# Moving layer 1's adaLN products from TensorE in the mixers to VectorE in the dense feed-forward

## The chip, the cores and the metric

The kernel runs on one core of a Trainium2 chip. The metric is the device time of one execution in microseconds (us); less is better.

## The reference

Two layers of a conditioned decoder trunk, in float32, on 256 tokens of width 1024. Each layer has a mixer (retention, an S5 state-space layer and multi-head latent attention beside each other) and a feed-forward: dense in layer 0, the top 2 of 8 routed experts in layer 1. A vector `c` of length 1024 modulates both (adaLN):

```python
cond = jax.nn.silu(c)
for layer in range(DEPTH):
    mod = (cond @ ada_w[layer] + ada_b[layer])[:, None, :]      # ada_w[layer]: 1024 x 6144
    sh_m, sc_m, gt_m, sh_f, sc_f, gt_f = jnp.split(mod, 6, axis=-1)
    h = rms_norm(x, norm_pre_mix[layer]) * (1.0 + sc_m) + sh_m
    y = hybrid_mixer(h, ...)
    x = x + gt_m * rms_norm(y, norm_post_mix[layer])
    h = rms_norm(x, norm_pre_ffn[layer]) * (1.0 + sc_f) + sh_f
    y = swiglu(h, ...) if layer % 2 == 0 else routed_ffn(h, ...)
    x = x + gt_f * rms_norm(y, norm_post_ffn[layer])
```

The change concerns `cond @ ada_w[1]`, a vector times a matrix of 24 MB.

## The kernel before

**Stages.** One program, in this order: the layer-0 mixer (to about 209 us), the dense feed-forward of layer 0 (to about 454), the layer-1 mixer with routing (to about 610), and the experts (to the end). There is no loop at run time; every instruction is written out, and each engine runs its own list in order. The lists come out of the order in which the Python code emits work.

**Loads.** All weights come as 1 MB pieces (`st`, 128x2048) into five staging buffers (`NS = 5`). A first, dry pass over the code notes the order in which pieces are asked for; `pump` then issues each load, from SP's queue, in that order, as soon as a buffer has been given back (`done`). A piece that is held long holds up all loads behind it.

**Weight splits.** A weight piece is split in halves of 128x1024 (128x896 for some of the input projection): ScalarE casts the high part (`wh`, L273), VectorE subtracts for the low part (`wl`, L274), up to five halves ahead (`NH = 5`); the second half's split gives the staging buffer back. Each product is then three matmuls: in `first` L1305 to L1307, elsewhere L733 to L735 (`mm3`).

**adaLN pieces.** `ada_steps(l, u)` gives ten steps for a third `u` of a layer's modulation: eight pieces, `total` and `fin`. The piece `k` takes 128 rows of `ada_w`; four matmuls (L474) multiply it by `c` (32 equal columns `c32`) and sum it up in a bank of PSUM. `total` adds the bias and multiplies by a gain on VectorE; `fin` turns the row into columns with four small matmuls (L490) and sends rows to all partitions. The steps stand in `self.queue`; `bg` takes the next one. The mixers call it at the letter B of their order strings `ORDER0`, `ORDER1`; at a mixer's end what is left over `keep` is run. In before, four pieces of (1,0) run at the end of the layer-0 mixer and four at the entry of the feed-forward (`self.bg(4)`), its `total` and `fin` in the first chunk; the steps of (1,1) and (1,2) run at the entry of the layer-1 mixer and inside it. The `fin` of (1,2) is followed by `fold_router` (L1380 to L1384).

**Mixer parts that are named.** `turn_x` (L681) transposes the tokens 0 to 127 (t=0) or 128 to 255 (t=1) with a diagonal `dg` (L674) that holds the norm; `hh`, `hl` are the parts of the normed input. In the attention (MLA), ScalarE copies the scores (`pe`, L1111), VectorE masks them and takes the maximum, ScalarE takes the exponential (L1118), PE transposes it (L1129), ScalarE copies that (`pT`, L1130), and PE multiplies by the values (L1136).

**Dense feed-forward.** Seven chunks `c` of 512 hidden columns. For each: `first('fg', c)`, Silu, `first('fu', c)`, the product `sg` and its parts `hTh`, `hTl`, and then `down(c - 1)`, which adds the chunk before into four banks. `down_last(6)` comes after the loop, with the post norm of the first 128 tokens. Meanwhile `adv` runs `s5_prep(1)`, in which GpSimd prepares the S5 layer of layer 1 with some small VectorE operations (`s5q`, `wp`, `s5r`, `R`).

Of the kernel before, what the change touches and what calls it, by code (L numbers as in the profile page):

```python
# [226 lines left out]
class Kernel:  # L227
# [226 lines left out]
    def ada_steps(self, l, u):  # L454
# [4 lines left out]
        def piece(k):  # L459
            def f():  # L460
                if k == 0:
                    state['p'] = self.bank("d")
                    if u == 0:
                        self.m4 = self.adp.tile([128, 512], F32, name="m4")
                        src = self.a['post_gain'][l]
                        self.nc.gpsimd.dma_start(self.m4, src[:, None, :].to_broadcast([4, 32, 512]))
                        if l == 0:
                            self.load_bias(0, 0)
                    if (l, u) != (L - 1, 2):
                        self.load_bias(*((l, u + 1) if u < 2 else (l + 1, 0)))  # L470
                key = ('ada', l, u, k)
                st, = self.stream.get(key, self.a['ada_w'][l, u, k], (1, 2048))
                for g in range(4):
                    self.T.matmul(state['p'][32 * g:32 * g + 32, :], self.c32[:, k, :],  # L474
                                  st[:, 0, g * 512:(g + 1) * 512], start=(k == 0), stop=(k == 7),
                                  skip_group_check=True)
                self.stream.done(key)
            return f

        def total():  # L480
            r = state['r'] = self.b4.pop((l, u))
            self.V.tensor_add(r, state['p'], r)
# [3 lines left out]
        def fin():  # L486
            r = state['r']
            pcs = self.bank("b")
# [787 lines left out]
    def ffn_dense(self, l, side=None):  # L1276
# [13 lines left out]
        def adv(n):  # L1290
            for _ in range(n):
                if side is not None:
                    next(side, None)

# [24 lines left out]
        def down(c):  # L1319
            for i in range(2):  # L1320
# [6 lines left out]
                self.w_done(key)  # L1327
            hT.pop(c)
# [15 lines left out]
        for c in range(NC):  # L1344
# [6 lines left out]
            adv(1)  # L1351
            pu = first('fu', c)
# [8 lines left out]
            adv(1)  # L1361
            if c == 0:
                self.bg()
            else:
# [3 lines left out]
                adv(2)  # L1368
        down_last(NC - 1)
# [514 lines left out]
    def run(self, upto=9):  # L1884
        tc = self.tc
        with ExitStack() as ctx:
# [11 lines left out]
            with ExitStack() as c5:  # L1898
# [18 lines left out]
                with ExitStack() as c1:  # L1917
                    self.pools(c1, dict(h8=2, f4=6, f2=6, f1=3))
                    self.queue += self.ada_steps(1, 2)
# [12 lines left out]
    def first_layer(self, upto):  # L1932

        with ExitStack() as c1:
            self.pools(c1, dict(h8=2, f4=6, f2=6, f1=3))
            self.setup()
            self.queue = self.ada_steps(0, 0) + self.ada_steps(0, 1) + self.ada_steps(0, 2) \
                + self.ada_steps(1, 0)
            self.keep = 6
# [7 lines left out]
        with ExitStack() as c1:  # L1947
            self.pools(c1, dict(h8=2, f4=4, f2=8, f1=1))
            self.load_layer(1, self.nc.gpsimd)
            side = self.s5_prep(1, self.G, self.G, self.G)  # L1950
            self.queue += self.ada_steps(1, 1)
            self.ffn_dense(0, side)
# [27 lines left out]
```

## Time and profile before

| | |
|---|---|
| median of 3 runs | 1485.74 us (1483.95 to 1491.18) |
| the profiled execution, its own time | 1491.5 us |
| its span, first to last instruction | 1489.7 us |
| mean granted clock of TensorE | 0.968 of full speed |

Each run is one execution. The profile is of one execution whose time is that in the second line; all rows below are from it. A mean of a whole span hides that stages have different limits, so rows are given by stretch or instruction.

### The profile page before, as it was taken

How to read it: one execution, taken by the hardware profiler on the slowest of the kernel's cores; microseconds unless marked ns; L12 is line 12 of the kernel's file. 1: busy time of each engine (PE TensorE's matmuls, PEld its weight loads, DVE VectorE, ACT ScalarE, POOL GpSimd, SP SyncE). 2: the span in 40 equal slices, each digit the busy share in tenths (PEclk: the TensorE clock that was granted, in tenths of full speed). 3: DMA queues.
4: the chain of work that ended last, by engine and by line, in shares of the span. 5: the costliest groups of instructions: out<-in, count | busy, mean ns of one | idle time of the engine just before them, and what ended most of it. 6: DMA issues, size and time to landing. Idle time of an engine off the chain costs nothing. (4 is left out here: it accounts for less than half of the span.)

```text
span 1489.7 us, 21982 instructions
## 1 busy us (share of the span) xinstructions
PE 1390.6 (93%) x8563; PEld 1042.6 (70%) x8563; DVE 848.3 (57%) x1201; ACT 675.4 (45%) x936; POOL 108.9 (7%) x108
## 2 busy tenths in 40 slices
PE   4799789999998999999999999999999998999995
PEld 1676579999997867665687887755687655687652
DVE  4763556656565546313898898522797403897302
ACT  1423444444445244113787877412676202786101
POOL 3201010515021001000000000000000000000000
PEclk9899999999999999799999999999999999999998
DMA  9667794545556484699999998999999999999995
GB/s 305 245 232 277 270 311 183 183 170 172 190 196 242 183 348 184 243 424 424 425 424 403 346 375 334 365 415 425 424 425 378 365 424 425 424 425 354 376 425 207
DMA packets 70078, 482.23 MB, mean 324 GB/s; under 512 B 9800, under 2 KB 10056, under 8 KB 13008
## 3 DMA queue, kind: packets, MB, share of 16 engines
q1 hardware_dynamic: 65952, 473.69, 80.2%
q0 software_dynamic: 3024, 4.75, 1.2%
q10 hardware_dynamic: 992, 2.33, 0.5%
q8 instruction: 69, 1.13, 0.3%
q14 instruction: 41, 0.34, 0.1%
HBM read 479.66 MB, written 1.06 MB: 323 GB/s over the span
## 5 line engine op out<-in xcount | busy, mean ns | idle before, releaser
L274 DVE TENSOR_TENSOR wl<-st,wh 128x1024 fp32r<-128x1024 f32 x464 | 569.6, 1248 | 192.9 <-ACT wh L273 170.0
L273 ACT CAST wh<-st 128x1024 fp32r<-128x1024 f32 x464 | 482.9, 1052 | 274.8 <-PE a L1306 86.4
L733 PE MATMUL a<-wh,xgh 128*128 128x512 f32 x448 | 180.5, 403 | 0.0
L734 PE MATMUL a<-wl,xgh 128*128 128x512 f32 x448 | 177.3, 396 | 2.7 <-DVE wl L274 2.7
L735 PE MATMUL a<-wh,xgl 128*128 128x512 f32 x448 | 176.7, 394 | 0.0
L1593 PE MATMUL a<-st,xs 128*64 128x256 f32 x1344 | 155.1, 381 | 0.9 <-DMA st<-in_mu 0.9
L1593 PEld LDWEIGHTS a<-st,xs 128*64 128x64 f32 x1344 | 95.4, 137 | 57.4 <-issue 12.4
L1305 PE MATMUL a<-hh,wh 128*128 128x256 f32 x448 | 128.2, 286 | 1.9 <-ACT hh L710 1.2
L1743 ACT ACTIVATE sg<-a 128x256 f32<-128x256 f32 (+1 forms) x56 | 27.3, 488 | 224.1 <-PE a L1593 224.1
L1754 DVE TENSOR_TENSOR h<-sg,a 128x256 f32<-128x256 f32 (+1 forms) x56 | 30.8, 551 | 172.1 <-PE a L1593 130.1
L1306 PE MATMUL a<-hl,wh 128*128 128x256 f32 x448 | 127.6, 285 | 0.4 <-DVE hl L711 0.4
L1307 PE MATMUL a<-hh,wl 128*128 128x256 f32 x448 | 127.4, 284 | 0.0
L1610 PE MATMUL b<-st,hts 128*64 128x512 f32 x448 | 110.7, 618 | 13.8 <-ACT hts L1602 9.9
L733 PEld LDWEIGHTS a<-wh,xgh 128*128 128x128 f32 x448 | 85.6, 191 | 22.2 <-issue 2.8
L734 PEld LDWEIGHTS a<-wl,xgh 128*128 128x128 f32 x448 | 85.7, 191 | 21.0 <-DVE wl L274 4.1
L735 PEld LDWEIGHTS a<-wh,xgl 128*128 128x128 f32 x448 | 85.6, 191 | 18.5
L1305 PEld LDWEIGHTS a<-hh,wh 128*128 128x128 f32 x448 | 86.6, 193 | 2.9 <-ACT hh L710 1.4
L1306 PEld LDWEIGHTS a<-hl,wh 128*128 128x128 f32 x448 | 86.6, 193 | 0.8 <-DVE hl L711 0.6
L1307 PEld LDWEIGHTS a<-hh,wl 128*128 128x128 f32 x448 | 86.7, 194 | 0.0
L1610 PEld LDWEIGHTS b<-st,hts 128*64 128x64 f32 x448 | 34.4, 141 | 73.2 <-issue 52.2
L474 PE MATMUL d<-st,c 128*32 128x512 f32 x384 | 53.4, 656 | 23.3 <-DMA st<-in_ada_w 12.1
L337 POOL TENSOR_TENSOR pss<-pss,mhalf 128x1 f32<-128x1 f32 x8 | 5.2, 649 | 890.1 <-DVE pss L336 890.1
(424 smaller groups left out, 1993.7 us busy)
## 6 DMA issues: line engine op xcount, KB each, us to landing
st<-in_mg SPq DMA_DIRECT2D x112, 1024.0 KB, 12.9
st<-in_mu SPq DMA_DIRECT2D x112, 1024.0 KB, 11.6
st<-in_md SPq DMA_DIRECT2D x112, 1024.0 KB, 12.7
st<-in_ada_w SPq DMA_DIRECT2D x48, 1024.0 KB, 7.8
st<-in_fg SPq DMA_DIRECT2D x14, 1024.0 KB, 4.8
st<-in_fu SPq DMA_DIRECT2D x14, 1024.0 KB, 4.8
st<-in_fd SPq DMA_DIRECT2D x14, 1024.0 KB, 4.7
st<-in_w_out SPq DMA_DIRECT2D x8, 1024.0 KB, 7.2
```

The costliest lines, as they stand in the source:

```text
L273: self.S.copy(hi, src)
L274: (E or self.V).tensor_sub(lo, src, hi.bitcast(F32))
L474: self.T.matmul(state['p'][32 * g:32 * g + 32, :], self.c32[:, k, :], st[:, 0, g * 512:(g + 1) * 512], start=(k == 0), stop=(k == 7), skip ...
L733: self.T.matmul(out, xh, wh, start=start, stop=False, skip_group_check=True)
L734: self.T.matmul(out, xh, wl, start=False, stop=False, skip_group_check=True)
L735: self.T.matmul(out, xl, wh, start=False, stop=stop, skip_group_check=True)
L1305: T.matmul(o, wh[:, k, fs], hh[:, kk], start=st, stop=False, skip_group_check=True)
L1306: T.matmul(o, wh[:, k, fs], hl[:, kk], start=False, stop=False, skip_group_check=True)
L1307: T.matmul(o, wl[:, k, fs], hh[:, kk], start=False, stop=(kk == 7), skip_group_check=True)
L1593: self.T.matmul(p[64 * t:64 * t + 64, :256], x[:, 4 * i + k], w[:, k, 256 * t:256 * t + 256], start=(i == 0 and k == 0), stop=(i == 1 and ...
L1610: self.T.matmul(y[64 * i:64 * i + 64, :], ht[:, f % 2, s], ws[i][:, f], start=(first and f == 0), stop=(last and f == 3), skip_group_check ...
L1754: V.tensor_mul(h, sg, pu[:, :w])
```

## The change

The 24 pieces of layer 1 leave the queue of the two mixers. `ada_steps` gets a second form (`vec=True`), in which a piece is one VectorE instruction on 128x2048: the first one multiplies by `c` (one number for each partition), the seven behind it multiply and add to a running tile `ada` (`SCALAR_TENSOR_TENSOR`). `total` then sums over the partitions with four matmuls 32x512 against ones. 29 steps are handed to `ffn_dense`, which takes one at each of the new `step` calls and the rest ahead of `down_last`; the `fin` of (1,2) alone goes on into the layer-1 mixer. The layer-0 mixer's queue ends with layer 0's own steps, `keep` is 0, and one pool gets a third 8 KB buffer for one of 2 KB less.

```diff
--- before.py
+++ after.py
@@ -451,7 +451,8 @@
         t = self.b4[l, u] = self.adp.tile([128, 512], F32, name="b4", bufs=2)
         self.nc.gpsimd.dma_start(t, self.a['ada_b'][l, u][:, None, :].to_broadcast([4, 32, 512]))
 
-    def ada_steps(self, l, u):
+    def ada_steps(self, l, u, vec=False):
 
         state = {}
         gs = slice(64 * (u - 1), 64 * u)
@@ -459,7 +460,7 @@
         def piece(k):
             def f():
                 if k == 0:
-                    state['p'] = self.bank("d")
+                    state['p'] = None if vec else self.bank("d")
                     if u == 0:
                         self.m4 = self.adp.tile([128, 512], F32, name="m4")
                         src = self.a['post_gain'][l]
@@ -470,6 +471,14 @@
                         self.load_bias(*((l, u + 1) if u < 2 else (l + 1, 0)))
                 key = ('ada', l, u, k)
                 st, = self.stream.get(key, self.a['ada_w'][l, u, k], (1, 2048))
+                if vec:
+                    c = self.c32[:, k, 0:1]
+                    if k == 0:
+                        state['a'] = self.wkt([128, 2048], "ada")
+                        self.V.tensor_scalar(state['a'], st[:, 0], c, None, op0=OP.mult)
+                    else:
+                        self.V.scalar_tensor_tensor(state['a'], st[:, 0], c, state['a'], op0=OP.mult, op1=OP.add)
+                    return self.stream.done(key)
                 for g in range(4):
                     self.T.matmul(state['p'][32 * g:32 * g + 32, :], self.c32[:, k, :],
                                   st[:, 0, g * 512:(g + 1) * 512], start=(k == 0), stop=(k == 7),
@@ -479,13 +488,18 @@
 
         def total():
             r = state['r'] = self.b4.pop((l, u))
+            if vec:
+                state['p'] = self.bank("a")
+                for g in range(4):
+                    self.T.matmul(state['p'][32 * g:32 * g + 32, :], self.ones[:, :32],
+                                  state['a'][:, g * 512:(g + 1) * 512], start=True, stop=True, skip_group_check=True)
             self.V.tensor_add(r, state['p'], r)
             if u:
                 self.V.tensor_mul(r[gs], r[gs], self.m4[gs])
 
         def fin():
             r = state['r']
-            pcs = self.bank("b")
+            pcs = self.bank("a" if vec and u < 2 else "b")
             for i in range(4):
                 self.T.matmul(pcs[:, 4 * i:4 * i + 4], r[:, i * 128:(i + 1) * 128], self.kc[:, C_E4:C_E4 + 4],
                               start=True, stop=True)
@@ -1273,7 +1287,7 @@
         p = self.ffn_args(name, c, i, e)
         return (p[0],) + tuple(self.w_piece(*p))
 
-    def ffn_dense(self, l, side=None):
+    def ffn_dense(self, l, side=None, steps=()):
 
         V, S, T = self.V, self.S, self.T
         hh, hl = self.parts_of_h()
@@ -1291,6 +1305,11 @@
             for _ in range(n):
                 if side is not None:
                     next(side, None)
+
+        def step(n=1):
+            for _ in range(n):
+                if steps:
+                    steps.pop(0)()
 
         def first(name, c):
             p = [self.bank("a"), self.bank("a")]
@@ -1325,6 +1344,7 @@
                     if f == 1:
                         self.w_half(key)
                 self.w_done(key)
+                step()
             hT.pop(c)
 
         def down_last(c):
@@ -1349,6 +1369,7 @@
             if c == 0:
                 self.bg()
             adv(1)
+            step()
             pu = first('fu', c)
             th = self.wkt([128, 4, 256], "hTh", F32R)
             tlo = self.wkt([128, 4, 256], "hTl", F32R)
@@ -1359,6 +1380,7 @@
                 V.tensor_sub(tlo[:, 2 * b:2 * b + 2], v, th[:, 2 * b:2 * b + 2].bitcast(F32))
             hT[c] = (th, tlo)
             adv(1)
+            step(2 if c == 0 else 1)
             if c == 0:
                 self.bg()
             else:
@@ -1366,6 +1388,7 @@
                     ys.extend([[self.bank("b"), self.bank("d")], [self.bank("b"), self.bank("b")]])
                 down(c - 1)
                 adv(2)
+        step(len(steps))
         down_last(NC - 1)
 
 
@@ -1916,7 +1939,6 @@
                 self.phase += 1
                 with ExitStack() as c1:
                     self.pools(c1, dict(h8=2, f4=6, f2=6, f1=3))
-                    self.queue += self.ada_steps(1, 2)
                     self.keep = 0
                     self.mixer(1, ORDER1, {})
                     self.end_post()
@@ -1934,9 +1956,8 @@
         with ExitStack() as c1:
             self.pools(c1, dict(h8=2, f4=6, f2=6, f1=3))
             self.setup()
-            self.queue = self.ada_steps(0, 0) + self.ada_steps(0, 1) + self.ada_steps(0, 2) \
-                + self.ada_steps(1, 0)
-            self.keep = 6
+            self.queue = self.ada_steps(0, 0) + self.ada_steps(0, 1) + self.ada_steps(0, 2)
+            self.keep = 0
             self.mixer(0, ORDER0, dict(Z=self.s5_prep(0, self.V, self.G, self.V), N=self.ch_start()))
         if upto == 1:
             return
@@ -1945,11 +1966,12 @@
             self.NC = 2
         self.phase += 1
         with ExitStack() as c1:
-            self.pools(c1, dict(h8=2, f4=4, f2=8, f1=1))
+            self.pools(c1, dict(h8=3, f4=4, f2=7, f1=1))
             self.load_layer(1, self.nc.gpsimd)
             side = self.s5_prep(1, self.G, self.G, self.G)
-            self.queue += self.ada_steps(1, 1)
-            self.ffn_dense(0, side)
+            last = self.ada_steps(1, 2, True)
+            self.ffn_dense(0, side, self.ada_steps(1, 0, True) + self.ada_steps(1, 1, True) + last[:-1])
+            self.queue += last[-1:]
             self.drain(side)
         if upto in (2, 12):
             return
```

`order` below means the list in which an engine's instructions stand; `x4` is four alike in a row.

ScalarE in the attention part of the layer-0 mixer, before: the exponentials of the first 128 tokens' scores, two casts of `w_out` (`wh`), then the copies `pe` of the next scores.

```order
L1118 ACT_TABLE_LOAD
L1118 ACTIVATE pe_1202,sm<-pe_1202,mx 128x128 x4
L273 CAST wh<-st 128x1024 x2
L1111 COPY pe_1256<-b 128x2x128 x2
L1118 ACTIVATE pe_1256,sm<-pe_1256,mx 128x256 x4
L1130 COPY pT_1286<-b 128x512
L273 CAST wh<-st 128x1024 x2
L772 ACTIVATE ch<-a,pc 128x256 x2
```

The same place after:

```order
L1132 ACT_TABLE_LOAD
L1132 ACTIVATE pe_1202,sm<-pe_1202,mx 128x128 x4
L273 CAST wh<-st 128x1024 x4
L1125 COPY pe_1266<-b 128x2x128 x2
L273 CAST wh<-st 128x1024
L1132 ACTIVATE pe_1266,sm<-pe_1266,mx 128x256 x4
L1144 COPY pT_1300<-b 128x512
L786 ACTIVATE ch<-a,pc 128x256 x2
```

Two of the casts that stood behind the copy of `pT` now stand ahead of the copies of `pe`, and a fifth ahead of the exponentials.

VectorE in the last chunk of the feed-forward and up to its post norm, before (`wl` are splits, `s5q`, `wp`, `s5r`, `R` are S5 preparation, `pyg` is the post norm):

```order
L549 TENSOR_TENSOR s5q_1985<-wp 128x16
L550 TENSOR_TENSOR s5q_1986<-wp 128x16
L551 TENSOR_TENSOR wp<-s5q_1985,s5q_1986 128x16
L552 TENSOR_SCALAR wp<-wp 128x8
L274 TENSOR_TENSOR wl<-st,wh 128x1024 x4
L549 TENSOR_TENSOR s5q_1985<-wp 128x16
L550 TENSOR_TENSOR s5q_1986<-wp 128x16
L551 TENSOR_TENSOR wp<-s5q_1985,s5q_1986 128x16
L552 TENSOR_SCALAR wp<-wp 128x8
L657 TENSOR_TENSOR s5r<-s5r 128x8
L658 TENSOR_TENSOR s5r<-s5r 128x8
L660 COPY R_4074<-s5r 128x512
```

The same place after; ahead of these rows stand, after the last `hTl` and four S5 rows, one more `SCALAR_TENSOR_TENSOR` on `ada` and two `wl`. The row behind the last one is the bias sum of `total` of (1,2):

```order
L480 SCALAR_TENSOR_TENSOR ada<-st,c_108,ada 128x2048
L274 TENSOR_TENSOR wl<-st,wh 128x1024 x2
L480 SCALAR_TENSOR_TENSOR ada<-st,c_108,ada 128x2048
L563 TENSOR_TENSOR s5q_1939<-wp 128x16
L564 TENSOR_TENSOR s5q_1940<-wp 128x16
L565 TENSOR_TENSOR wp<-s5q_1939,s5q_1940 128x16
L566 TENSOR_SCALAR wp<-wp 128x8
L671 TENSOR_TENSOR s5r<-s5r 128x8
L672 TENSOR_TENSOR s5r<-s5r 128x8
L674 COPY R_4122<-s5r 128x512
L675 MEMSET R_4122 128x8
L480 SCALAR_TENSOR_TENSOR ada<-st,c_108,ada 128x2048
```

Four of the multiply-and-add instructions now stand between the last `hTl` and the post norm, with the splits and the S5 rows among them.

PE between the last `down` of the loop and `down_last`, after (before, the same rows follow each other without the L494, at L733 to L735):

```order
L747 MATMUL b<-wh,hTh 128x512
L748 MATMUL b<-wl,hTh 128x512
L749 MATMUL b<-wh,hTl 128x512
L494 MATMUL a<-ada,kc 32x512 x4
L747 MATMUL b<-wh,hTh 128x512
L748 MATMUL b<-wl,hTh 128x512
L749 MATMUL b<-wh,hTl 128x512
L747 MATMUL b<-wh,hTh 128x512
```

The four matmuls of `total` (L494) read `ada`; the matmuls of `down_last` stand behind them.

SP's loads for the last chunk, before (`fg`, `fu`, `fd` are the gate, up and down weights, `win_*` the input projection of the next mixer):

```order
L189 DMA st<-in_fg 128x2048 x2
L189 DMA st<-in_fu 128x2048 x2
L189 DMA st<-in_fd 128x2048 x4
L189 DMA st<-in_win_u 128x2048
L189 DMA st<-in_ada_w 128x2048 x5
L189 DMA st<-in_win_m 128x1792 x2
L189 DMA st<-in_win_q 128x2048 x2
```

The same place after:

```order
L189 DMA st<-in_fg 128x2048 x2
L189 DMA st<-in_ada_w 128x2048
L189 DMA st<-in_fu 128x2048 x2
L189 DMA st<-in_ada_w 128x2048
L189 DMA st<-in_fd 128x2048
L189 DMA st<-in_ada_w 128x2048
L189 DMA st<-in_fd 128x2048
L189 DMA st<-in_ada_w 128x2048 x2
L189 DMA st<-in_fd 128x2048 x2
L189 DMA st<-in_win_u 128x2048
L189 DMA st<-in_win_m 128x1792 x2
```

The pieces `ada_w` stand between the weights' loads, two of them ahead of the last two `fd`, and no longer between the loads of the input projection.

## Rows read from the trace of the kernel before

**Rows 1.** The page's busy times: us (share of the span) xinstructions.

```profile
PE 1390.6 (93%) x8563; PEld 1042.6 (70%) x8563; DVE 848.3 (57%) x1201; ACT 675.4 (45%) x936; POOL 108.9 (7%) x108
```

**Rows 2.** Busy time by stretch: PE, PEld, DVE, ACT, POOL, then PEclk, DMA share, GB/s.

```profile
209.00:443.00 234.00, 232.82 (x1688) 220.46 (x1689) 139.66 (x180) 105.81 (x122) 53.65 (x40) 0.99 0.52 186
460.00:500.00 40.00, 36.20 (x247) 31.82 (x248) 19.00 (x36) 17.19 (x32) 1.30 (x2) 0.91 0.64 227
610.00:1470.00 860.00, 831.14 (x4616) 585.58 (x4616) 496.62 (x541) 420.01 (x496) 0.70 (x1) 0.98 0.97 397
```

**Rows 3.** Costliest groups: the adaLN pieces; busy, mean ns, idle before.

```profile
L474 PE MATMUL d<-st,c 128*32 128x512 f32 x384 | 53.4, 656 | 23.3 <-DMA st<-in_ada_w 12.1
```

**Rows 4.** Timeline, end of layer-0 mixer, PE and DVE: start, us, engine, line.

```profile
203.13 1.63 PE L474 MATMUL d<-st,c 128*32 128x512 f32 x8 [2.30 <-DMA st<-in_ada_w]
204.68 3.10 PE L681 MATMUL a<-dg,x 128*128 128x128 f32 x16
...
200.92 0.29 DVE L674 TENSOR_SCALAR dg<-kc,rs 128x128 f32<-128x128 f32 x1 [0.66 <-POOL rs L337]
```

**Rows 5.** Timeline, MLA part of the layer-0 mixer, ACT and PE.

```profile
149.63 1.99 ACT L273 CAST wh<-st 128x1024 fp32r<-128x1024 f32 x2 [2.06 <-DMA st<-in_w_out]
151.53 0.64 ACT L1111 COPY pe<-b 128x256 f32<-128x256 f32 x2
...
157.88 2.08 PE L1136 MATMUL b<-vv,pT 128*128 128x128 f32 x8 [6.19 <-ACT pT L1130]
```

**Rows 6.** Timeline, DVE and POOL: sizes of operations, and one beside GpSimd.

```profile
450.37 1.41 DVE L764 SCALAR_TENSOR_TENSOR x<-pyg,pss,x 128x512 f32<-128x512 f32 x2
...
594.46 1.28 DVE L1422 SCALAR_TENSOR_TENSOR xnl<-x,rs,xnh 128x1024 fp32r<-128x1024 f32 x1
...
281.83 2.29 DVE L274 TENSOR_TENSOR wl<-st,wh 128x1024 fp32r<-128x1024 f32 x1 [1.06 <-ACT wh L273]
...
281.76 1.28 POOL L597 TENSOR_TENSOR pre<-q,q 128x512 f32<-128x512 f32 x1
```

**Rows 7.** Timeline, feed-forward, end of the fourth `down`, DVE and PE.

```profile
368.68 0.69 DVE L1359 TENSOR_TENSOR hTl<-sg,hTh 128x512 fp32r<-128x512 f32 x1 [0.69 <-ACT hTh L1358]
...
373.95 0.28 PE L1305 MATMUL a<-hh,wh 128*128 128x256 f32 x1
```

**Rows 8.** Timeline, last feed-forward chunk, DVE and PE; issue to landing of loads.

```profile
430.43 1.23 DVE L274 TENSOR_TENSOR wl<-st,wh 128x1024 fp32r<-128x1024 f32 x1 [1.65 <-ACT wh L273]
...
434.45 0.68 DVE L1356 TENSOR_TENSOR sg<-sg,a 128x512 f32<-128x512 f32 x1
...
437.79 0.69 DVE L1359 TENSOR_TENSOR hTl<-sg,hTh 128x512 fp32r<-128x512 f32 x1 [0.69 <-ACT hTh L1358]
...
445.53 0.17 DVE L549 TENSOR_TENSOR s5q<-wp 128x16 f32<-128x16 f32 x1
...
448.55 0.07 DVE L661 MEMSET R<- 128x8 f32 x1
...
443.05 0.39 PE L733 MATMUL b<-wh,hTh 128*128 128x512 f32 x1
...
st<-in_fd SPq DMA_DIRECT2D x14, 1024.0 KB, 4.7
```

**Rows 9.** Timeline, layer-1 mixer, PE.

```profile
460.03 2.02 PE L681 MATMUL a<-dg,x 128*128 128x128 f32 x16 [0.57 <-DVE dg L674]
...
466.24 0.54 PE L835 MATMUL a<-hh,wh 128*128 128x256 f32 x1 [3.20 <-ACT hh L710]
...
508.44 2.78 PE L474 MATMUL d<-st,c 128*32 128x512 f32 x24
...
558.68 1.16 PE L1136 MATMUL b<-vv,pT 128*128 128x128 f32 x8 [0.16 <-ACT pT L1130]
...
567.45 1.05 PE L490 MATMUL b<-kc,b 128*128 128x4 f32 x8 [0.83 <-ACT pT L1130]
...
569.90 3.76 PE L1136 MATMUL b<-vv,pT 128*128 128x128 f32 x16
```

## The prediction

> **What bounds the kernel now.** I read the page's busy times first: TensorE (PE) is busy 93% of the span, VectorE (DVE) 57% [rows 1]. That is a mean over stages, so I read next the busy times by stretch. In the dense feed-forward (209 to 443 us) PE is busy 232.82 of 234 us while DVE is busy 139.66, ScalarE about half and the DMA engines 0.52 of the time. In the expert stage (610 to 1470 us) PE is busy 831 of 860 us and the DMA share is 0.97 [rows 2]. The expert stage isn't touched by the change; whatever moves ahead of it moves its start and so the end. What the change can win or lose lies in the first 610 us, in two parts whose limits differ: in the feed-forward each microsecond put on PE is paid, and DVE has about 94 us to spare; in the two mixers PE has holes, in which a piece costs nothing.
>
> The third view is the costliest groups: the 48 adaLN pieces (8 matmuls in the profile each, for 4 in the code) take 53.4 us of PE, with 23.3 us of idle time before them, about half of it waits for their own load [rows 3]. A piece alone is about 1.07 us. So 24 pieces are some 26 us of PE time at most, and the timeline must say which of them PE waits for.
>
> **Part 1, the end of the layer-0 mixer (about -2).** Removed: eight pieces. Three stand in line in the output product and cost about 1.0 each; a fourth lies in a wait for DVE. The last four stand between the two transposes `turn_x`. The diagonal `dg` for the second is ready at 200.92 + 0.29 = 201.2, but the transpose starts at 204.68, because a piece ahead of it waited 2.30 us for its load [rows 4]. That is 3.5 us won; with the three, 6.5.
>
> Given back: ScalarE's order changes (the first two fences of the section on the change). With the pieces gone from the load queue the `w_out` loads come earlier in the order, so four casts `wh`, not two, stand ahead of the copy `pe` that feeds the softmax. Before, that copy came 1.9 us after the first of the casts, at 151.53; the chain behind it (scale, maximum, exponential, transpose) ended with PE waiting 6.19 us for `pT` at 157.88 [rows 5]. So this chain is the path here. The two extra casts belong to the second `w_out` load, which takes an earlier slot of SP's queue than now; from the slots I estimate its landing at 153.3 (before, a piece's load sat there), so `pe` comes near 155.4, 3.9 late, and with one `wl` more on DVE before the maximum (1.23) I subtract 4.7 altogether. Net -1.8; the bounds are -6.5 (load early, casts hidden) and 0.
>
> **Part 2, the feed-forward (about +32).** Added on DVE: 24 products of 128x2048. The trace has no such row. Nearest: the same operation at 128x512 takes 1.41 us for two, at 128x1024 it takes 1.28 [rows 6]. The slope is 0.575 per 512 columns, which gives 2.43; twice the wider row is 2.56, four slopes without any fixed part 2.3. I take 2.4. For 24 that is 57 us, inside DVE's 94 us of room, so over six chunks it is hidden: the stage's 84 half-pieces of weights (seven chunks of 12) last PE 2.9 us each, and splits (`wh`, `wl`) stand up to five halves ahead. The price if that cover goes is rival 1. Their loads, 24 MB on SP's queue, add less than half to what the DMA engines move there at 0.52. The pieces' bias rows and the finishes' rows go by POOL's queue, behind its S5 work, but are read eight steps later or in the next stage: nothing.
>
> Added on PE: three sums `total` at about 1.05 each (four matmuls 32x512, like a piece) = 3.2, and the finish of (1,1), four transposed columns of each row, about 1.0. They are in line in a stretch where PE is never idle, so both are paid.
>
> New waits of PE on DVE. `total(1,1)` stands at the end of `down(3)`, which PE ended at 373.95 in the trace. DVE ends its hT chain there at 368.68 + 0.69 = 369.4 [rows 7]; behind it stand a product (2.4), two `wl` (2.4) and the last product (2.4), so 376.5: PE waits 2.5.
>
> `total(1,2)` is the large one: `step(len(steps))` puts it on PE right before `down_last`, and PE takes its matmuls in order. On DVE it stands behind everything in the fence on VectorE: four products, the remaining `wl` and the S5 operations. Queued behind the waiting matmuls on PE are the 48 of `down_last`, whose weights are split by then, and all that follows it. I follow DVE's queue with the trace's durations. The last chunk's loads: five staging buffers, four of them held by `ada` pieces and `fd51`, so the load of `fd60` is issued only when the split at 430.43 ends (431.7), and lands after 4.7 (the median landing of such loads) at 436.4 [rows 8]. Cast 1.05 and `wl` 1.23: 438.7. The hT chain takes 4.0 us (434.45 to 438.48 in the trace) [rows 8]: 442.7. Four S5 operations, 0.6: 443.3. First product: 445.7; it frees the buffer for `fd61`, which lands at 450.4. `wl`: 446.9. Cast and `wl` of `fd61`: 452.7. Second product 455.1; two `wl` 457.5; third product 459.9; the remaining S5 operations 3.1 (445.53 to 448.62 in the trace) 463.0; fourth product 465.4. PE ended `down(5)` at 443.05 [rows 8]. So PE stands still for some 22 us. If the loads did not hold anything, the same queue without the gap for `fd61` and with `fd60` at its old time ends at about 456: a stall of 13, the lower bound of this term; the upper is 27, with the products stretched by GpSimd (below).
>
> After such a stop PE comes back at the lower of its two clock levels: after the idle time at the entry of layer 1 the stretch 460 to 500 ran at a granted clock of 0.91 [rows 2], which is 18% of 40 us at half speed, a loss of 3.6 us; here I take 3. Sum of part 2: 3.2 + 1.0 + 2.5 + 22 + 3 = +31.7.
>
> **Part 3, the layer-1 mixer (about -4.6).** Five pieces at its entry are hidden now: PE waits after them for `dg` (0.57) and for `hh` (3.20) [rows 9], so that removing them brings nothing. But the order changes: the loads no longer wait behind pieces, so three casts and three `wl` of 128x896 (about 1.1 each by the 128x1024 row) stand ahead of the second half's chain, and the finish of (1,2) with the fold of the router goes in before the second `turn_x` (about 2). I take +4.7.
>
> Inside, eight pieces stand where PE is never idle (0.93 each by the row of three: 2.78), with one `L490` of about 1: 8.4; against that I set 1.5, an estimate for three more `wl` that come ahead of the S5 scan on DVE: -6.9. Three more pieces are hidden in the softmax chain (PE waits for `pT` behind them, 0.16). At the end the finish and the router's fold move PE's L1136 from 567.45 to 569.90 [rows 9]: -2.4. Together 4.7 - 6.9 - 2.4 = -4.6; bounds -9.3 (entry hidden) and +1 (interior gains eaten by the new order of `wl`).
>
> **The sum.** -1.8 + 31.7 - 4.6 = +25.3 us. The profiled execution took 1491.5, 5.8 above the median 1485.74 of the runs (inside what they vary, 1483.95 to 1491.18); the difference is laid on the median: 1511.0.
>
> **A rule of the skill that speaks against the change.** The row: a `wl` of 128x1024 took 2.29 us while GpSimd ran a tensor operation of 1.28 us that had begun 0.07 us earlier [rows 6]; undisturbed it takes 1.23 [rows 8]. That is 1.06 lost, not a share but nearly the whole of GpSimd's instruction. The Trainium skill, "SBUF — State Buffer", section "Who interferes with whom", says that a VectorE instruction with two SBUF inputs and a GpSimd instruction that reads SBUF exclude each other for a whole instruction. By this rule, which the trace agrees with (1.28 + 1.23 - 0.07 = 2.44 against 2.29), every added product, which reads a staged piece and its running sum, pays for each GpSimd operation it meets. What that would make of the sum is the first rival, which is worked out from rows alone.
>
> **Rivals.**
> 1. *VectorE becomes the bound of the feed-forward.* GpSimd is busy 53.65 us in 209 to 443 [rows 2]. With 57 us of products DVE is at 197 of 234. Busy more than four fifths of the time, it would meet up to 45 of GpSimd's 54 us: 242, more than there is, though a part of that is in the 139.66 already. Then `wl` comes late for PE at some chunks as well. It decides when one chunk of 34 us has more than about 34 us of DVE work; the price is 5 to 15 more: 1516 to 1526. Against: five halves of splits ahead, about 11 us of slack.
> 2. *The tail stall is small and gains and losses cancel.* The change would do on balance nothing if the last products finished about when `down(5)` does. Sum without the 22 and the 3: +0.3, 1486; with the lower stall 13: 1502. For it: over 209 to 443 DVE has room. Against: the queue above is counted row by row, and four products alone are 9.6 us behind a chain ending at 442.7.
> 3. *Faster.* The stall is hidden as in 2, and the mixers give their upper bounds: -6.5 at the end of layer 0 (no late `pe`), -9.3 in layer 1, +6.7 of sums, finish and wait in the feed-forward: -9.1, 1477. It decides if the last two steps find their data ready. For it: PE is the busiest engine and 24 pieces leave it. Against: in the mixers it waited beside most of them.
>
> **How the numbers follow.** The forecast (stall 13 to 27, 1500 to 1520) gets 0.60, rival 1 0.12, rival 2 0.15, rival 3 0.13. About 0.5%, 7.4 us, is what a measurement of this kernel can tell from no change: faster (under 1478.3) 0.13, same 0.15, slower (over 1493.2) 0.72. The range 1486 to 1526 reaches down to rival 2's own time and up over rival 1; it leaves out rival 3 and the edges of 1 and 2. The forecast's own range is 1500 to 1520.
>
> **What would show it.** In the changed kernel's timeline, PE's four matmuls of `total(1,2)` wait about 22 us for `ada` from DVE, with DVE's four products spread between 443 and 465 and a wait for the cast of `fd61` in the midst; the products take 2.4 us, up to 3.6 beside GpSimd. `total(1,1)` waits 2.5 us, `total(1,0)` hardly. The second `turn_x` of layer 0 starts right after `dg`, and PE's wait for `pT` before the first L1136 grows by some 4 to 5. The expert stage keeps its length. It is wrong if the wait before `down_last` is under 10 us, or if chunks 1 to 5 of the feed-forward get longer than their sums explain.

## The result and the profile after

| | before | after |
|---|---|---|
| median | 1486.2 us (1483.95 to 1491.18, 4 runs) | 1559.97 us (1555.85 to 1562.78, 4 runs) |
| ratio | 1 | 1.048, 95% interval 1.045 to 1.051 |
| span of the profiled execution | 1489.7 us | 1558.6 us |

The change costs 74 us, about three times what was forecast (25); the range that was given ended at 1526. The page of the changed kernel has TensorE (PE) doing a little less work than before and idle for more of the span; compare [rows 1].

```profile
span 1558.6 us, 21695 instructions
PE 1387.2 (89%) x8395; PEld 1050.4 (67%) x8395; DVE 909.9 (58%) x1225; ACT 674.5 (43%) x936; POOL 123.9 (8%) x108
```

Where the 69 us of span went is read by stage. A stage is bounded by PE's first matmul of `first` and by its `turn_x` transposes in the timeline. The feed-forward is cut once more, at the end of the last `first`: ahead of it are the seven chunks, behind it the tail (`down(5)`, the last sum, `down_last`).

| stretch | before | after | difference | forecast |
|---|---|---|---|---|
| to the first matmul of the feed-forward | 209.0 | 211.8 | +2.8 | -1.8 |
| chunks 0 to 6 | 223.1 | 262.3 | +39.2 | +5.6 |
| tail | 21.8 | 52.3 | +30.5 | +26.1 |
| layer-1 mixer | 137.4 | 134.4 | -3.0 | -4.6 |
| routing, experts, end | 898.4 | 897.8 | -0.6 | 0 |

(Of the forecast's 31.7 for the feed-forward two sums, 2.1, the finish, 1.0, and a wait, 2.5, lie in the chunks, the rest in the tail.) The mixers and the tail are within 5 us of the forecast. The chunks are not: they hold 34 of the 44 us that were missed.

The busy times by stretch of the kernel after, from the layer-0 mixer's end on, one row for each stage of the table (columns as in [rows 2]):

```profile
157.00:211.80 54.80, 37.77 (x185) 30.58 (x185) 27.10 (x54) 25.49 (x61) 6.66 (x10) 0.82 0.38 144
211.80:474.10 262.30, 236.09 (x1664) 221.21 (x1665) 183.09 (x192) 99.35 (x116) 68.15 (x42) 0.93 0.65 235
474.10:526.40 52.30, 24.61 (x107) 18.67 (x107) 28.77 (x37) 10.57 (x17) 9.33 (x8) 0.74 0.48 169
526.40:660.80 134.40, 118.51 (x813) 97.19 (x812) 73.15 (x140) 57.69 (x124) 7.83 (x11) 0.91 0.37 134
660.80:1558.60 897.80, 847.60 (x4718) 600.19 (x4716) 514.13 (x583) 432.38 (x523) 3.66 (x5) 0.97 0.94 384
```

In the chunks VectorE (DVE) is busy 183 of 262 us. By that share it still has room, as before; yet PE has 26 us of holes there, where it had 1 before:

```profile
209.00:432.10 223.10, 221.92 (x1640) 211.41 (x1641) 131.42 (x168) 100.56 (x116) 49.74 (x37) 0.99 0.52 188
```

So the share doesn't tell; the waits do. The holes make 25 of the chunks' 39.2 us. The other 14.2 are PE's own busy time (236.1 against 221.9): about 3 were forecast for the sums and the finish, and the rest goes with the granted clock, 0.93 in place of 0.99. Behind a wait of 5.4 us, which is shown below, PE ran at its lower clock level; the window of the kernel after:

```profile
258.00:266.00 8.00, 4.51 (x21) 4.51 (x22) 5.70 (x4) 0.66 (x1) 0.00 (x0) 0.50 0.87 340
```

PE's waits over the span of the kernel after (what it waited for, us in total, times, longest):

```profile
PE a L494 <- DVE ada L480: 35.6, 2, 27.7
PE b L1150 <- ACT pT L1144: 14.9, 4, 12.2
PE a L1326 <- DVE wl L274: 11.3, 2, 5.9
PE d L1406 <- DVE rbs L1404: 8.2, 1, 8.2
PE a L1324 <- ACT sg L1368: 4.0, 2, 3.6
```

The first row is the two sums that were forecast to wait: 27.7 ahead of `down_last` (forecast 22, upper bound 27) and 7.9 for `total(1,1)` (forecast 2.5). The third is the one that the prediction held to be covered: weight splits that come late to PE. The fifth has the same root: the Silu (`sg`) that PE waits 3.6 us for stands on ScalarE behind a cast that waited for its load.

How they come late is seen where chunk 0 goes over into chunk 1. The timeline of the kernel after, SP, then ACT, DVE and PE:

```profile
234.50 4.15 SPq L189 DMA_DIRECT2D st<-in_fu  x2
257.94 0.33 SPq L189 DMA_DIRECT2D st<-in_ada_w  x1
...
246.19 1.05 ACT L273 CAST wh<-st 128x1024 fp32r<-128x1024 f32 x1 [9.16 <-DMA st<-in_fu]
...
247.28 1.23 DVE L274 TENSOR_TENSOR wl<-st,wh 128x1024 fp32r<-128x1024 f32 x1 [8.98 <-ACT wh L273]
248.42 0.68 DVE L1377 TENSOR_TENSOR sg<-sg,a 128x512 f32<-128x512 f32 x1
...
255.57 4.73 DVE L480 SCALAR_TENSOR_TENSOR ada<-st,c,ada 128x2048 f32<-128x2048 f32 x2
260.22 3.49 DVE L274 TENSOR_TENSOR wl<-st,wh 128x1024 fp32r<-128x1024 f32 x3
...
261.49 0.58 PE L1326 MATMUL a<-hh,wl 128*128 128x256 f32 x1 [5.41 <-DVE wl L274]
```

A `fu` load issued at 234.5 lands only at 246 (11.2 us is the median of the two `fu` loads here, 6.3 of all in this feed-forward); ScalarE's cast and VectorE's `wl` wait 9 us for it, and behind them in VectorE's order wait the chunk's product `sg`, its parts and then the two `ada` products, which start at 255.57. The pieces of these two, and a third that was issued at 233.37, hold three of the five staging buffers until then, so SP issues no load from 238.7 to 257.9. The next splits stand behind the products, and PE waits 5.4 us for `wl`. It is a ring: a held buffer makes a load late, the late load blocks VectorE, and VectorE then frees the held buffer late. What SP waited for in the feed-forward of the kernel after has the two halves of it:

```profile
SPq L189 <- DVE ada L480: 135.4, 19, 19.2
SPq L189 <- DVE wl L274: 128.4, 42, 22.3
```

The sum of these waits is no measure of the loss, since SP waited for most of the feed-forward before the change too, for splits alone:

```profile
SPq L189 <- DVE wl L274: 221.5, 42, 10.9
```

The second thing in the chunks is GpSimd. The products of the kernel after in the view of the tile `ada` (ns min/median/max):

```profile
L480 DVE SCALAR_TENSOR_TENSOR ada<-st,c,ada x21: 2337/2347/3377, 255.6 to 509.6; 128x2048 f32<-128x2048 f32 x21
```

One of them in the timeline, beside a GpSimd operation:

```profile
287.25 3.21 DVE L480 SCALAR_TENSOR_TENSOR ada<-st,c,ada 128x2048 f32<-128x2048 f32 x1
...
288.29 3.08 POOL L597 TENSOR_TENSOR q<-s5par,s5F 128x512 f32<-128x512 f32 x1
```

A product takes 2.35 us alone, near the estimate (2.4); those that meet GpSimd take 2.6 to 3.4.

The tail, VectorE and PE. Its queue is in the order of the forecast, but starts about 4 us later relative to PE: the split at 483.91, which waited for its load, ends as PE ends `down(5)` (485.2), and the forecast had it 4.4 us ahead of that:

```profile
483.91 1.23 DVE L274 TENSOR_TENSOR wl<-st,wh 128x1024 fp32r<-128x1024 f32 x1 [8.50 <-ACT wh L273]
...
489.58 2.80 DVE L480 SCALAR_TENSOR_TENSOR ada<-st,c,ada 128x2048 f32<-128x2048 f32 x1
...
498.65 1.23 DVE L274 TENSOR_TENSOR wl<-st,wh 128x1024 fp32r<-128x1024 f32 x1 [4.72 <-ACT wh L273]
...
509.57 3.22 DVE L480 SCALAR_TENSOR_TENSOR ada<-st,c,ada 128x2048 f32<-128x2048 f32 x1
...
512.94 1.94 PE L494 MATMUL a<-ada,kc 128*32 128x512 f32 x8 [27.69 <-DVE ada L480]
```

### The profile page after: what moved, and what is told of

The parts are those of the page before. It is cut to its first block, busy times and chain, and to the rows that moved or that the text cites. A ratio compares the mean times of both kernels' runs of the same rounds, so it can differ in the third digit from the quotient of the medians.

```text
span 1558.6 us, 21695 instructions
## 1 busy us (share of the span) xinstructions
PE 1387.2 (89%) x8395; PEld 1050.4 (67%) x8395; DVE 909.9 (58%) x1225; ACT 674.5 (43%) x936; POOL 123.9 (8%) x108
## 5 line engine op out<-in xcount | busy, mean ns | idle before, releaser
L1326 PE MATMUL a<-hh,wl 128*128 128x256 f32 x448 | 131.5, 293 | 11.3 <-DVE wl L274 11.3
L1324 PE MATMUL a<-hh,wh 128*128 128x256 f32 x448 | 132.6, 296 | 6.5 <-ACT sg L1368 4.0
L1325 PE MATMUL a<-hl,wh 128*128 128x256 f32 x448 | 131.2, 293 | 0.9 <-DVE hl L725 0.9
L1326 PEld LDWEIGHTS a<-hh,wl 128*128 128x128 f32 x448 | 90.7, 202 | 11.7 <-DVE wl L274 11.7
L1324 PEld LDWEIGHTS a<-hh,wh 128*128 128x128 f32 x448 | 90.8, 203 | 9.5 <-ACT sg L1368 4.4
L1325 PEld LDWEIGHTS a<-hl,wh 128*128 128x128 f32 x448 | 90.7, 202 | 1.3 <-DVE hl L725 1.2
L480 DVE SCALAR_TENSOR_TENSOR ada<-st,c,ada 128x2048 f32<-128x2048 f32 x21 | 55.1, 2623 | 0.1
```

The lines of the kernel that those rows point to most:

```text
L480: self.V.scalar_tensor_tensor(state['a'], st[:, 0], c, state['a'], op0=OP.mult, op1=OP.add)
L1324: T.matmul(o, wh[:, k, fs], hh[:, kk], start=st, stop=False, skip_group_check=True)
L1325: T.matmul(o, wh[:, k, fs], hl[:, kk], start=False, stop=False, skip_group_check=True)
L1326: T.matmul(o, wl[:, k, fs], hh[:, kk], start=False, stop=(kk == 7), skip_group_check=True)
```

## The experiments

Two theories for the 34 us that the chunks lost beyond the forecast. **S**: pieces that wait for their turn hold staging buffers, and late weight loads do the rest. **D**: VectorE has too much work, above all beside GpSimd (rival 1). Each experiment starts from the changed kernel. For a whole run two stretches are compared, taken from its own timeline as in the table above. `e9_only11`, `e10_gap` and `e12_entry` have 6, 10 and 12 executions, the others one each, and a profile is always of one. The whole time of the kernel before varied from 1478 to 1497 us, so single whole times tell less than the stretches.

### No loads, or thin products

`e1_no_loads`: the products read `x`, which lies in SBUF, in place of the loaded piece.

```diff
-                st, = self.stream.get(key, self.a['ada_w'][l, u, k], (1, 2048))
+                if vec:
+                    st = self.x.rearrange("p t d -> p (t d)")[:, None]
+                else:
+                    st, = self.stream.get(key, self.a['ada_w'][l, u, k], (1, 2048))
...
-                    return self.stream.done(key)
+                    return
```

> The 24 pieces are not loaded; the products read the resident x instead (same size, other numbers), so VectorE does all its work and no piece holds a staging buffer. Theory S (pieces that wait in the five staging buffers hold up the weight loads, late weights hold up VectorE, and that holds the pieces longer): the stalls in the first three chunks go, the tail stall shrinks from 28 to about 13, 1510 to 1520. Theory D (57 us of products on VectorE, stretched by GpSimd, are too much whatever the loads do): 1545 to 1560. My own forecast of the queue without load holding was 1502.

Measured: the chunks take 238.8 us (262.3 in the kernel after, 223.1 before), the tail 40.7 (52.3; 21.8). Its whole time, 1696.42, isn't to be read: with other modulation the routing and expert stage does other work (5296 matmuls in place of 4718) and is 173 us longer. In its feed-forward all VectorE work is there, and 35 of the 70 us are gone. The wait ahead of `down_last` is 14.9. S holds for half of the loss.

`e2_thin`: loads and order stay, each multiply-and-add works on 64 columns.

```diff
-                        self.V.scalar_tensor_tensor(state['a'], st[:, 0], c, state['a'], op0=OP.mult, op1=OP.add)
+                        self.V.scalar_tensor_tensor(state['a'][:, :64], st[:, 0, :64], c, state['a'][:, :64], op0=OP.mult, op1=OP.add)
```

> The loads and the order of all instructions stay, but each multiply-and-add works on 64 of the 2048 columns, so some 50 us of VectorE time are left out. Theory S: a piece still holds its buffer until its place in VectorE's queue, behind splits that wait for loads; most of the loss stays, 1530 to 1550. Theory D: nearly all of it goes, 1495 to 1515.

Measured: 1532.21 us; chunks 246.1, tail 42.7. With nearly no product time on VectorE the feed-forward still takes 44 us longer than before, as S expects. D alone is out. But 26 us went with the product time, so D has a part.

### Loads three places later

`e3_late3`: all work stays. In the load order a piece of layer 1 stands three weight pieces later than where the code asks for it. (Weights are split up to five halves ahead of their use, pieces are used at once; a common order therefore loads a piece long before its turn.)

```diff
+def later(order, n):
+    at, w = [], 0
+    for e in order:
+        ada = e[0][0] == 'ada' and e[0][1] == 1
+        at.append(w + n - 0.5 if ada else w)
+        w += not ada
+    return [order[i] for i in sorted(range(len(order)), key=lambda i: (at[i], i))]
...
+    dry.stream.order = later(dry.stream.order, 3)
```

> All work stays; each piece is loaded three weight pieces later in the load order, near the time at which its product runs. Theory S: buffers are held for a shorter time, the stalls of chunks 1 and 2 and the hold of the last down weights go, 1515 to 1530. Theory D: no change, 1550 to 1565. If pieces then come too late for VectorE's queue, new stalls of 5 to 10.

Measured: 1520.55 us (1486.65 for the kernel before, run beside it). Chunks 238.7, tail 40.8: both as without any loads (238.8 and 40.7). So the whole price of the loads, 35.1 us, was the time for which they held buffers; none of it shows as a price of the traffic. The windows of its chunks and tail:

```profile
209.30:448.00 238.70, 230.27 (x1664) 215.70 (x1665) 184.05 (x193) 100.52 (x116) 70.28 (x42) 0.97 0.73 264
448.00:488.80 40.80, 25.94 (x108) 19.65 (x107) 27.94 (x35) 10.59 (x17) 9.34 (x8) 0.79 0.51 187
```

The DMA share went up to 0.73 and VectorE is as busy as before the edit (184), in 24 us less. The wait ahead of `down_last` is 14.9, near the 13 that the prediction's queue gave without the hold.

`e5_thin_late3`: both edits.

> Both edits: pieces loaded three weights later, and each multiply-and-add on 64 of 2048 columns (the rest of the product left out). If held buffers and VectorE time are the whole loss in the feed-forward, its stretch is the 245 us of before plus about 5 for the sums and the finish on TensorE, 250 to 256; if something third is at work (the extra instructions in the order, DMA traffic), over 265.

Measured: 1499.84 us (1494.77 for the kernel before, run beside it); chunks 227.4, tail 32.9, together 260.3, which lies between the two ranges. The chunks are 4.3 us over before, a little under the sum of the prediction's terms for them (5.6), and PE's busy time in them is 225.6 at a granted clock of 0.99: against the 236.1 of the kernel after, some 10 us of the chunks' loss was the lower clock behind the waits. The tail is 11 over before; 6.8 of that is a wait for its sum, which still stands behind splits and S5 operations on VectorE, about 2 are the sum itself, and about 2 PE's other work at a clock of 0.84. There is no third cause of size.

### GpSimd moved away

`e11_s5`: on `e3_late3`, the S5 preparation is run ahead of the feed-forward, with its time added there.

```diff
             side = self.s5_prep(1, self.G, self.G, self.G)
+            self.drain(side)
```

> On the late-loaded version, GpSimd's S5 preparation runs ahead of the feed-forward and not beside it; its time is added there and isn't to be compared, the feed-forward's own stretch is. If meeting GpSimd stretches VectorE enough to reach TensorE (rival 1): 268 to 274 in place of 279.5, no product over 2.4 us. If TensorE's stalls come from the order alone: 277 to 280.

Measured: chunks 228.2, tail 34.4, together 262.6, 16.9 us less than `e3_late3`, and 5 less than the lower end of what was expected of rival 1. The window of its chunks:

```profile
263.40:491.60 228.20, 224.88 (x1616) 211.68 (x1617) 155.49 (x134) 97.61 (x107) 1.83 (x3) 0.98 0.74 276
```

Its products in the view of the tile `ada`:

```profile
L480 DVE SCALAR_TENSOR_TENSOR ada<-st,c,ada x21: 2344/2347/2352, 296.6 to 509.4; 128x2048 f32<-128x2048 f32 x21
```

No product takes over 2.352 us, and VectorE's busy time in the chunks falls from 184 to 155. Added up one by one (they overlap a little), the splits are 15.5 us shorter and the products 5.3, and 10.0 us of VectorE's own small S5 operations are gone, which the edit takes away as well. So the 16.9 are those and the meetings together, and the run can't tell what each is worth to PE. The Trainium skill, "SBUF — State Buffer", section "Who interferes with whom", says that a VectorE instruction with two SBUF inputs and a GpSimd instruction that reads SBUF contend for a pair of ports that is locked for one of them at a time. The runs agree that both pay: GpSimd's own busy time rose from 108.9 us [rows 1] to 123.9 on the page after, and fell to 90.5 on the page of `e11_s5`, with the same 108 instructions.

### The tail

`e4_tail`: on the kernel after, `step(len(steps))` stands behind `down_last`.

```diff
-        step(len(steps))
         down_last(NC - 1)
+        step(len(steps))
```

> The last two steps (the last product and the sum of the third row) run after down_last in place of before it. If the wait before down_last is a loss of its own: 27 us less and about 5 for the sum at the new place, 1535 to 1541. If down_last's weights and hT parts are late anyway (they stand in the same queue): 1548 to 1555.

Measured: 1557.53 us, near the second range; tail 45.3 in place of 52.3. Where the one wait was, PE now waits 4.1 us for `wl` in `down_last` and 14.2 for the sum behind it. Moving the last sum helps little while the products ahead of it are late.

`e6_spread`: on `e3_late3`, a fifth step in each chunk from chunk 1 on, so that only the last sum is left in chunk 6.

```diff
-            step()
+            step(2 if c else 1)
             pu = first('fu', c)
```

> On the late-loaded version, two steps instead of one behind each gate product from chunk 1 on, so that all products but none of the tail's are done by chunk 5 and only the last sum is left in chunk 6. If the tail stall (14.9 us there) is only a matter of place: 1502 to 1508. If VectorE has no room for a fifth product a chunk (the theory that it is the bound): stalls come up in chunks 1 to 5 instead, 1515 to 1530.

Measured: 1519.04 us (1494.77 for the kernel before, run beside it); the tail is 21.9, as before the change, and PE doesn't wait there; the chunks are 247.7, 9.0 more than in `e3_late3`: waits of 2.1 us for a sum and of 6.0 and 2.7 for finishes came up. The feed-forward is 10 us shorter than in `e3_late3`; the whole time hides that, since the feed-forward began 4.5 us later. Both halves of what was expected are in it. The tail's 19 us are a matter of place. And VectorE has no room for a fifth product beside S5 in chunk 1: from 253.3 to 291.6 it is busy 36.6 of 38.3 us, and the waits of 2.1 and 6.0 stand right behind.

### Fewer rows on VectorE

`e7_pe10`: on `e3_late3`, row (1,0) goes back to PE (queue and `keep` as before).

```diff
-            self.queue = self.ada_steps(0, 0) + self.ada_steps(0, 1) + self.ada_steps(0, 2)
-            self.keep = 0
+            self.queue = self.ada_steps(0, 0) + self.ada_steps(0, 1) + self.ada_steps(0, 2) \
+                + self.ada_steps(1, 0)
+            self.keep = 6
...
-            self.ffn_dense(0, side, self.ada_steps(1, 0, True) + self.ada_steps(1, 1, True) + last[:-1])
+            self.ffn_dense(0, side, self.ada_steps(1, 1, True) + last[:-1])
```

> On the late-loaded version, row (1,0) goes back to TensorE in the layer-0 mixer and at the feed-forward's entry, as before; (1,1) and (1,2), 16 products, stay on VectorE and are done by chunk 4. The wait for pT in the layer-0 mixer goes back from 11 us to about 6; the feed-forward pays two sums and no tail stall, 250 to 258; the layer-1 mixer keeps its gain of 2. 1488 to 1497. If the end of layer 0 gains from having no pieces (my part 1), 1492 to 1500.

Measured: 1501.54 us (1494.77 for the kernel before, run beside it), a little above the range; chunks 234.1, tail 21.9. The wait for `pT` in the layer-0 mixer is 6.0 us, as before the change; in all runs with the new queue it is 11.0 to 12.4. But the feed-forward begins at 211.4, no earlier than in those runs (207.1 to 213.8): what PE waits less for `pT` it seems to pay in pieces.

`e10_gap`: as `e7_pe10`, with two empty places ahead of each sum and one ahead of the first finish.

```diff
+            mid, gap = self.ada_steps(1, 1, True), [lambda: None]
+            self.ffn_dense(0, side, mid[:8] + 2 * gap + mid[8:9] + gap + mid[9:] + last[:8] + 2 * gap + last[8:9])
```

> Rows (1,1) and (1,2) on VectorE, late loads, and two empty places between the last product of a row and its sum, one more ahead of the finish. TensorE's waits for those sums (4.5 and 1.3 us where they follow at once) go, and the loss of clock behind them: feed-forward 248 to 251, not 256; layer-1 mixer 134 to 136 as in the other versions; in all 0.999 to 1.004 of before. If the waits only move to another place: 1.006 to 1.010.

Measured: 1495.28 us, 1.004 of before (1.002 to 1.006). Its chunks, tail and layer-1 mixer:

```profile
209.90:438.20 228.30, 225.72 (x1664) 212.69 (x1665) 175.39 (x190) 100.69 (x116) 62.41 (x40) 0.99 0.71 262
438.20:460.10 21.90, 21.90 (x100) 18.06 (x99) 16.11 (x29) 10.51 (x17) 9.38 (x8) 1.00 0.41 138
460.10:593.10 133.00, 115.50 (x814) 95.45 (x814) 73.18 (x140) 57.47 (x124) 7.83 (x11) 0.94 0.37 135
```

Two of three rows on VectorE now cost the feed-forward 5.3 us and give the layer-1 mixer 4.4 back. Part of the 4.4 hangs on the granted clock in this profile: PE was busy for 115.5 us of the mixer at 0.94, and in `e7_pe10` for 118.7 us at 0.91 with the same work.

`e9_only11`: only (1,1) on VectorE; (1,2) on PE, in the places that (1,1) had at the entry.

```diff
+            mid, gap = self.ada_steps(1, 1, True), [lambda: None]
+            self.ffn_dense(0, side, mid[:8] + 2 * gap + mid[8:9] + gap + mid[9:])
+            self.queue += self.ada_steps(1, 2)
```

> A version meant to beat both: only row (1,1), 8 products, goes to VectorE in the feed-forward, with pieces loaded three weights later, two empty places ahead of its sum and one ahead of its finish; (1,0) and (1,2) stay on TensorE as before, (1,2) now in the places that (1,1) had at the entry of the layer-1 mixer. Feed-forward 247 to 249 (before 245), entry of layer 1 as before (6 us between the two turn_x), 6 to 9 less inside that mixer: 1479 to 1484, 0.995 to 0.999 of before. If the layer-1 mixer gains nothing because its holes move: 1.001 to 1.003.

Measured: 1504.89 us, 1.009 (1.007 to 1.012): a miss. The feed-forward was as expected (248.6) and the entry too (6.1 between the `turn_x`), but the layer-1 mixer took 146.6, 9 more than before. PE's busy time in it is the same as before (131.1 us) with 73 matmuls less, since the granted clock is 0.87 in it, 0.95 before; and it has a new wait of 5.6 us for `rg` from ScalarE. Which of the moved pieces brings the wait was not followed further.

### The entry of the layer-1 mixer

`e8_fin`: on `e3_late3`, twelve empty places in the queue ahead of the last finish.

```diff
-            self.queue += last[-1:]
+            self.queue += [lambda: None] * 12 + last[-1:]
```

> On the late-loaded version, the last finish and the router's fold run twelve places later in the layer-1 mixer's queue, not at its entry. The 8.2 us wait of TensorE for the fold at the entry goes; the second turn_x comes 6 to 7 us behind the first as before, not 11: 4 to 5 us less in that mixer, 1515 to 1517. If the splits ahead of dg hold the entry up anyway, under 1 us.

Measured: 1524.28 us. The second `turn_x` stands 9.1 us behind the first (11.3 in `e3_late3`, 6.1 before): the wait for the fold (8.2) turned into one of 7.1 for `dg`, which stands behind four splits on VectorE. The mixer took 138.8, 3.1 more. A miss.

`e12_entry`: `e10_gap` with four empty places there, and one split in place of four ahead of the post norm.

```diff
             for i in range(2):
-                self.w_done(ws[i][0])
+                self.w_done(ws[i][0], ahead=i)
```

> e10 with two changes at the layer-1 mixer's entry: behind down_last one split in place of four goes into the queues of ScalarE and VectorE ahead of the second half's post norm, and the last finish with the router's fold comes four places later, behind the second turn_x. If these two make the entry long (the second turn_x 11.4 us behind the first in e10, 6.1 before): 7 to 8 there, the mixer 128 to 131 in place of 133, in all 0.997 to 1.001 of before. If the fold or the splits only wait elsewhere, 132 to 134 and 1.003 to 1.005.

Measured: 1495.2 us, 1.004 (1.002 to 1.007). The entry is 8.1 us, near what was expected, but the mixer 135.5. PE's holes in it are 16.3 us, against 17.5 in `e10_gap`, so little of the wait was saved, and PE's busy time rose from 115.5 to 119.2, with the granted clock at 0.91 in place of 0.94; why the clock was lower was not followed. PE still waited for `dg`, as the row of its waits shows:

```profile
PE a L695 <- DVE dg L688: 6.2, 1, 6.2
```

No version beat the kernel before.

## Why the prediction was wrong

**The step that failed** is in part 2: "For 24 that is 57 us, inside DVE's 94 us of room, so over six chunks it is hidden". It was argued from a share of busy time and from splits standing ahead, and the piece's staging buffer was counted only in the tail, where four of five held buffers were noted. In the chunks the same holding costs 23.6 us (262.3 against 238.7 in `e3_late3`), and in the tail 11.5. The prediction's second sign of being wrong, chunks that get longer than their sums explain, is what came. The cover that the step named, splits up to five halves ahead, needs weights that have landed, and the held buffers make these late. The lower clock behind waits, which the prediction charged to the tail alone (3), is some 10 us of the chunks' loss; it is contained in these figures.

**Rival 1** (VectorE beside GpSimd) was true in part at the same time. Its price was 5 to 15; `e11_s5` gives 16.9 in all, 10.5 of it in the chunks (238.7 to 228.2), VectorE's small S5 operations included. Its condition, more than about 34 us of VectorE work in a chunk, came about in one: in `e3_late3` VectorE is busy 34.2 of the 35.9 us from 250.3 on. It was weighed as an alternative; it came on top. What is left of the chunks' loss is 5.1 us, against 5.6 from the terms for sums, finish and wait.

**The tail** was right in mechanism and near in size: forecast stall 22 (13 without the hold), measured 27.7 (14.9 in `e3_late3`). The term is too small by 6, of which about 4 are that VectorE's queue came into the tail late already. `total(1,1)` waited 7.9, not 2.5, and in `e3_late3` 4.5.

**A product's time** was 2.35 against 2.4. **The loads** were put at less than half of what the DMA engines moved in the feed-forward; 24 pieces are 25 MB, and 45 MB moved there before, so it is more than half. By `e3_late3` that cost nothing.

**Part 1**: its 4.7 is less than the two terms it names (3.9 and 1.23, together 5.1). PE's wait for `pT` did grow, from 6.2 [rows 5] to 12.2, and the second `turn_x` of layer 0 starts right behind its `dg`, as forecast. The net, -1.8, can't be told: the stage varies by 7 us over the runs, and 3 of the 9 us by which L1150 came late in the profile were there before the order differs.

**Part 3**: entry +5.3 (forecast +4.7), the rest of the mixer -8.2 (forecast -9.3). PE's wait for the fold there is 8.2, with four splits ahead of it. Right in mechanism; that the sum came within 2 us is in part luck, as the mixer took from 133.0 to 135.8 us over the runs in which it is the same.

**Rivals 2 and 3** (tail hidden) fail at the tail and at the chunks. With tail and chunks mended, and one row left on PE, `e10_gap` ends 0.4% above before, not at 1477: the feed-forward keeps 5.3 us of cost, and the layer-1 mixer gives no more than 4.4 back.

## What to carry to other kernels

A load that is asked for in order but used late takes a staging buffer out of the pipeline for all loads behind it: count for each new load how long it holds its buffer, before counting bandwidth or busy time. Give a load a place in the order by the time of its use; here that alone won 35 us. Idle time in an engine's share is not yet room: VectorE was idle 41% of the chunks before, but it takes its list in order, and an instruction put in line there delayed all behind it. Here a wait of PE cost twice, once as a hole and once by the lower clock behind it.

## What the runs showed of the hardware

`TENSOR_SCALAR` on 128x2048 in float32 took 1.28 us where `SCALAR_TENSOR_TENSOR` took 2.35; the row of the kernel after:

```profile
L478 DVE TENSOR_SCALAR ada<-st,c x3: 1278/1281/2068, 232.1 to 446.8; 128x2048 f32<-128x2048 f32 x3
```

The slowdown beside GpSimd goes both ways: its two 128x512 operations that began at 293.66 us take 2.5 us each, where before the two that began at 283.12 took 1.5 each, and in `e11_s5` eight of the same line take 1.05 on average.
